# Gates, branch projections and values by tokens, 512 channels at a time

## The chip, the cores and the metric

One core of a Trainium2 chip. The metric is the device time of one execution in microseconds, median of several runs. The granted clock of TensorE is given as a share of 2.4 GHz; it was 0.991 on average over the profiled span, and 1.00 in every stretch that this text speaks of.

## The reference, cut to what matters

One layer of a decoder on 256 positions (T) of 1,024 channels (D), all in float32. The part that the change touches is the token mixer:

```python
qa, ka, va, qd, kd, vd, b_gate, c_gate, hc, gate_logits = jnp.split(
    x @ w_in, split_points, axis=-1)
y_moba = moba_attention(...)                     # 512 wide, values va: 512
y_conv = b_gate * causal_dwconv(c_gate * hc, w_short_conv)   # 512 wide
y_dil = dilated_mixture(...)                     # 256 wide, values vd: 768
gates = jax.nn.sigmoid(gate_logits).reshape(b, s, N_BRANCH, D_MODEL)
merged = (gates[:, :, 0] * (y_moba @ w_moba_proj)
          + gates[:, :, 1] * (y_conv @ w_conv_proj)
          + gates[:, :, 2] * (y_dil @ w_dil_proj))
return merged @ w_mix_out
```

Behind it come a residual with layer norm, an MLP with a gated convolution (w_up, w_down), and a second residual with layer norm. The change leaves these as they are.

## The kernel before, in words

Every weight is read once from memory, in blocks of 2,048 float32 per partition (1 MB; some branch blocks are smaller), on SyncE's DMA queue (`load_next`, L111) into three `raw` buffers. A block is cut into pieces of 128x512. Each float32 operand of a matrix product is split into two rounded parts, h and l (`split`, L148): ScalarE copies h (L149), VectorE subtracts to get l (L150). A product of two split operands is three passes on TensorE (`mm3`, L198 to 202: h·h, h·l, l·h). Pieces are split in the order of use, up to 10 ahead (`LEAD`); a new block is loaded when the last piece of a block has been split.

The program is written as a chain of groups. A group fills one accumulator bank (`acc`, three in rotation, L60) and ends with `tick` (L155), which splits further pieces, then has the bank emptied (`consume`), then issues one entry of the list `side` (attention work that is strung between the groups). A scheduler may shift instructions a little within an engine's row. In order of the program:

- queries and keys, by channels (`project`, L209): the weight's 128 columns stay in the array, the 256 tokens of transposed x (xTh, xTl) move through it;
- values (L462 to 464), by tokens (`project_tokens`, L218): 128 tokens of x stay, 256 columns of the weight move. Three groups of 256 channels for the dilated attention, two for MoBA;
- short convolution, MoBA queries and keys, with the attention in between;
- gates and branches (L504 to 529), by channels, in four quarters d of 256 channels. In each, the three gates are projected (L509: ScalarE writes the sigmoid), then for both halves c of 128 channels the three branches with `take(5)` pieces: VectorE multiplies the product with the gate (L523) and adds (L525). `late` splits the gated sum, which has channels on partitions and so can stay in the array for the next product as it is;
- output projection w_mix_out (L597 to 622), by tokens, products of 512 columns into five `att` banks, then residual and layer norm; then the MLP.

Of the kernel before, what the change touches and what calls it, by code (L numbers as in the profile page):

```python
# [7 lines left out]
F32 = mybir.dt.float32  # L8
F32R = mybir.dt.float32r
I32 = mybir.dt.int32  # L10
BF16 = mybir.dt.bfloat16
AF = mybir.ActivationFunctionType
# [25 lines left out]
def trunk(ctx: ExitStack, tc, x, w_in, w_short_conv, w_moba_proj, w_dil_proj, w_conv_proj, w_mix_out,  # L38
# [18 lines left out]
    def buf(dt=F32, shape=(P, 512)):  # L57
        return act.tile(list(shape), dt, tag="b2", name=fresh("b"), bufs=B2)

    def acc(shape=(P, 512)):  # L60
        return ps.tile(list(shape), F32, tag="acc", name=fresh("acc"), bufs=3)
# [8 lines left out]
    def block(*parts):  # L70

        blocks.append(parts)

    def kview(w, c0, c1, k0=0, k1=None):
        k1 = w.shape[0] // P if k1 is None else k1
        return w[k0 * P:k1 * P, c0:c1].rearrange("(k p) c -> p k c", p=P)

    def columns(base, n):
        for b in range(n):
            c = base + 256 * b  # L80
            block(kview(w_in, c, c + 256))

    columns(DIL_Q, 3)
    columns(DIL_K, 3)
    columns(DIL_V, 3)
    columns(MOBA_V, 2)
    for b in range(2):
        columns(CONV_C + 256 * b, 1)
        columns(CONV_H + 256 * b, 1)
        columns(MOBA_Q + 256 * b, 1)  # L90
        columns(MOBA_K + 256 * b, 1)
    columns(CONV_B, 2)
    for d in range(4):
        for g in range(3):
            columns(GATE + g * D + d * 256, 1)
        c = d * 256
        block(kview(w_dil_proj, c, c + 256))
        block(kview(w_conv_proj, c, c + 256), kview(w_moba_proj, c, c + 256))
    for b in range(4):
        block(kview(w_mix_out, 0, D, 2 * b, 2 * b + 2))  # L100
    for j in range(0, NJ + 2, 2):
# [40 lines left out]
    def take(n):  # L142

        i = used[0]
        assert len(ready) >= i + n, (len(ready), i, n)
        return ready[i:i + n]
# [8 lines left out]
    def tick(n, consume=None, ahead=1):  # L155


        used[0] += n
        while late:
            late.pop(0)()  # L160
        prep(n + ahead)
        if consume:
            consume()
        if side:
            side.pop(0)()
# [32 lines left out]
    def mm3(o, ah, al, bh, bl, first, last):  # L198

        nc.tensor.matmul(o, ah, bh, start=first, stop=False)  # L200
        nc.tensor.matmul(o, ah, bl, start=False, stop=False)  # L201
        nc.tensor.matmul(o, al, bh, start=False, stop=last)  # L202

    def cut(w, k, c0, c1):

        c = (k % 2) * 256
        return [t[:, c + c0:c + c1] for t in w[k // 2]]

    def project(consume, xh=xTh, xl=xTl, ahead=1):  # L209

        w = take(4)
        for c in range(2):
            o = acc((P, T))
            for k in range(KT):
                mm3(o, *cut(w, k, c * P, c * P + P), xh[:, k, :], xl[:, k, :], k == 0, k == KT - 1)
            tick(2, lambda: consume(c, o), ahead)

    def project_tokens():  # L218

        w = take(4)  # L220
        vh, vl = buf(F32R, (P, 2, 256)), buf(F32R, (P, 2, 256))
        for t in range(2):
            s = slice(t * P, (t + 1) * P)
            o = acc((P, T))
            for k in range(KT):
                mm3(o, xTh[:, k, s], xTl[:, k, s], *cut(w, k, 0, 256), k == 0, k == KT - 1)
            tick(2, lambda: split(o, vh[:, t, :], vl[:, t, :]))
        return vh, vl
# [230 lines left out]
    yd = [buf(F32R, (P, 2, T)) for _ in range(2)]  # L459
    p, q = (dilated(c, dq, dk, dv, [t[:, c, :] for t in yd]) for c in range(2))  # L460
    side += [p[0], p[1], p[2], q[0], p[3], p[4], q[1], p[5], q[2], p[6], q[3], q[4], q[5], q[6]]
    for g in range(3):  # L462
        dv.append(project_tokens())
    mv = [project_tokens() for b in range(2)]

    conv, ymT = [], []
    for b in range(2):
# [34 lines left out]


    merged = []  # L504
    for d in range(4):
        gs = []
        for g in range(3):
            s = buf(F32, (P, 2, T))
            project(lambda c, o: nc.scalar.activation(s[:, c, :], o, AF.Sigmoid))  # L509
            gs.append(s)  # L510
        assert not side
        m = gs[2]
        h, l = buf(F32R, (P, 2, T)), buf(F32R, (P, 2, T))
        w = take(5)
        for c in range(2):
            for g, k0, n, ys in ((2, 0, 2, [yd]), (1, 2, 4, ycT), (0, 6, 4, ymT)):
                o = acc((P, T))
                for k in range(n):
                    yh, yl = ys[k // 2]
                    mm3(o, *cut(w, k0 + k, c * P, c * P + P), yh[:, k % 2, :], yl[:, k % 2, :], k == 0, k == n - 1)  # L520

                def merge():
                    nc.vector.tensor_mul(gs[g][:, c, :], o, gs[g][:, c, :])  # L523
                    if g < 2:
                        nc.vector.tensor_add(m[:, c, :], m[:, c, :], gs[g][:, c, :])  # L525

                tick({(0, 2): 0, (0, 1): 1, (0, 0): 1, (1, 2): 1, (1, 1): 1, (1, 0): 1}[c, g], merge)
            late.append(lambda c=c, m=m, h=h, l=l: split(m[:, c, :], h[:, c, :], l[:, c, :]))
        merged.append((h, l))


    half_c = const.tile([P, 1], F32, name="half_c")
# [67 lines left out]
    for t in range(2):  # L600
        for c0, c1, p in mo[t]:
            for k in range(2):
                row_products(p, merged[0], w, k, t, c0, c1, k == 0, False)
        tick(2)
    wm = []
    for b in (1, 2, 3):
        while len(ready) < used[0] + 4:
# [124 lines left out]
```

## Time and profile before

| | |
|---|---|
| median of 3 runs | 479.36 us (479.05 to 480.07) |
| the profiled execution | 479.29 us, span of its instructions 477.5 us |
| instructions | 9,121, of them 3,582 products on TensorE |
| bytes read from memory | 81.9 MB, 174 GB/s over the span |

PE is TensorE's products, PEld its weight loads (they overlap), DVE is VectorE, ACT is ScalarE, SP is SyncE. Products on TensorE are pipelined: the length shown for one is longer than the step to the next, so the step from start to start is to be read.

### The profile page before, as it was taken

The numbers are of one execution on the slowest core, as the hardware profiler recorded it, in microseconds if no ns is written. First come the engines' busy times: TensorE is split into PE (matmuls) and PEld (weight loads), VectorE is DVE, ScalarE is ACT, GpSimd is POOL, SyncE is SP. The second block draws the span as 40 slices with busy tenths as digits, with TensorE's granted clock in tenths as the row PEclk, the third lists the DMA queues.
The fourth block names the chain that finished last, engine by engine and source line by source line (L and its number), as shares of the span: only waits on it lengthen the run. The fifth ranks groups of instructions, "written<-read, shape, count | busy, mean of one in ns | idle before, by whom it ended". The sixth has DMA issues, their size and how long they took to land.

```text
span 477.5 us, 9121 instructions
## 1 busy us (share of the span) xinstructions
PE 466.5 (98%) x3582; PEld 450.6 (94%) x3582; DVE 360.3 (75%) x775; ACT 271.0 (57%) x579; POOL 10.4 (2%) x29
## 2 busy tenths in 40 slices
PE   7999999999999999999999999999999999999993
PEld 4999999999999999999999899999999999999983
DVE  6788996778989757484748866997867676786966
ACT  4767774737668645454545316866555565564710
POOL 1100000010100000000000000000000000000000
PEclk8999999999999999999999999999999999999997
DMA  8986555254451745656465914657465545637002
GB/s 265 359 253 189 178 177 177 89 176 131 136 161 41 231 144 182 195 165 211 153 220 200 311 49 151 243 175 265 127 227 176 178 177 188 221 122 244 21 2 88
DMA packets 69502, 83.51 MB, mean 175 GB/s; under 512 B 1688, under 2 KB 64852, under 8 KB 69460
## 3 DMA queue, kind: packets, MB, share of 16 engines
q1 hardware_dynamic: 69460, 82.94, 53.3%
q8 instruction: 28, 0.46, 0.4%
q14 instruction: 14, 0.11, 0.1%
HBM read 81.89 MB, written 1.05 MB: 174 GB/s over the span
## 4 chain that ended last, share of the span: by engine, by line
PE 97%; DMA 1%; DVE 1%; SPq 0%; ACT 0%; issue 0%; DVEq 0%
PE acc L200 24%; PE acc L202 24%; PE acc L201 24%; PE att L201 7%; PE att L200 7%; PE att L202 7%; PE att L266 2%; PE acc L439 1%; PE att L287 1%; DMA xs<-in_x_dram 1%; PE att L194 0%; DVE r L551 0%; SPq L124 0%; SPq L177 0%; PE acc L594 0%
## 5 line engine op out<-in xcount | busy, mean ns | idle before, releaser
L150 DVE TENSOR_TENSOR b<-raw,b 128x512 fp32r<-128x512 f32 x300 | 196.1, 687 | 38.0 <-ACT b L149 35.6
L149 ACT CAST b<-raw 128x512 fp32r<-128x512 f32 x300 | 169.3, 620 | 6.2 <-DMA raw<-in_w_in_dram 2.9
L200 PE MATMUL acc<-xTh,b 128*128 128x256 f32 x432 | 122.9, 284 | 0.0
L201 PE MATMUL acc<-xTl,b 128*128 128x256 f32 x432 | 122.2, 283 | 0.0
L202 PE MATMUL acc<-xTh,b 128*128 128x256 f32 x432 | 122.2, 283 | 0.0
L200 PE MATMUL acc<-x1Th,b 128*128 128x256 f32 x320 | 90.9, 284 | 0.0
L202 PE MATMUL acc<-x1Th,b 128*128 128x256 f32 x320 | 90.6, 283 | 0.0
L201 PE MATMUL acc<-x1Tl,b 128*128 128x256 f32 x320 | 90.5, 283 | 0.0
L200 PEld LDWEIGHTS acc<-xTh,b 128*128 128x128 f32 x432 | 82.8, 192 | 0.2
L201 PEld LDWEIGHTS acc<-xTl,b 128*128 128x128 f32 x432 | 82.9, 192 | 0.0
L202 PEld LDWEIGHTS acc<-xTh,b 128*128 128x128 f32 x432 | 82.9, 192 | 0.0
L201 PEld LDWEIGHTS acc<-x1Tl,b 128*128 128x128 f32 x320 | 61.4, 192 | 0.1
L200 PEld LDWEIGHTS acc<-x1Th,b 128*128 128x128 f32 x320 | 61.4, 192 | 0.1
L202 PEld LDWEIGHTS acc<-x1Th,b 128*128 128x128 f32 x320 | 61.4, 192 | 0.0
L629 DVE SCALAR_TENSOR_TENSOR b<-acc,fconv,b 128x255 f32<-128x255 f32 x80 | 38.5, 481 | 30.2 <-ACT b L627 29.2
L200 PE MATMUL att<-b,b 128*128 128x512 f32 (+1 forms) x170 | 58.9, 347 | 0.0
L201 PE MATMUL att<-b,b 128*128 128x512 f32 (+1 forms) x170 | 58.9, 347 | 0.0
L202 PE MATMUL att<-b,b 128*128 128x512 f32 (+1 forms) x170 | 58.7, 345 | 0.0
L149 ACT CAST b<-b 128x256 fp32r<-128x256 f32 x34 | 13.8, 408 | 46.8 <-DVE b L525 23.4
L627 ACT ACTIVATE b<-acc,fconv 128x256 f32<-128x256 f32 x40 | 22.6, 565 | 28.6 <-PE acc L202 28.6
L200 PEld LDWEIGHTS att<-b,b 128*128 128x128 f32 x170 | 32.2, 189 | 4.0
L202 PEld LDWEIGHTS att<-b,b 128*128 128x128 f32 x170 | 32.1, 189 | 4.0
(108 smaller groups left out, 625.0 us busy)
## 6 DMA issues: line engine op xcount, KB each, us to landing
raw<-in_w_in_dram SPq DMA_DIRECT2D x31, 1024.0 KB, 5.7
raw<-in_w_up_dram SPq DMA_DIRECT2D x22, 1024.0 KB, 5.4
raw<-in_w_down_dram SPq DMA_DIRECT2D x11, 1024.0 KB, 5.0
raw<-in_w_mix_out_dram SPq DMA_DIRECT2D x4, 1024.0 KB, 5.3
raw<-in_w_in_dram SPq DMA_DIRECT2D x8, 256.0 KB, 6.2
raw<-in_w_conv_proj_dram SPq DMA_DIRECT2D x4, 512.0 KB, 3.5
raw<-in_w_moba_proj_dram SPq DMA_DIRECT2D x4, 512.0 KB, 4.6
xs<-in_x_dram SPq DMA_DIRECT2D x4, 256.0 KB, 3.6
```

The source lines that it names most:

```text
L149: nc.scalar.copy(h, src)
L150: nc.vector.tensor_sub(l, src, h.bitcast(F32))
L200: nc.tensor.matmul(o, ah, bh, start=first, stop=False)
L201: nc.tensor.matmul(o, ah, bl, start=False, stop=False)
L202: nc.tensor.matmul(o, al, bh, start=False, stop=last)
L266: nc.tensor.matmul(o, qt, k[i][:, a, :], start=i == 0, stop=i == 1)
L287: nc.tensor.transpose(p[:, i, :], b, ident)
L439: nc.tensor.matmul(o[c], w[i][:, s:s + P], xt[:, k, :], start=k + i == 0 and xt is xTh, stop=k == KT - 1 and i == 1)
L627: nc.scalar.activation(v, o, AF.Identity, bias=w[3], scale=w[0])
L629: nc.vector.scalar_tensor_tensor(v[:, j:], o[:, :T - j], w[j], v[:, j:], op0=OP.mult, op1=OP.add)
```

## The change

Three places go from 256 to 512 columns:

- `wide` lays a weight out as two blocks of four rows of 128 by 512 columns; a piece is then one row k with 512 columns, where it was two rows with 256.
- `by_tokens` takes the place of `project` for gates and branches, and of `project_tokens` for four of the five value groups: 128 tokens of the input stay in the array, 512 columns of the weight move. It fills two banks at once, one for each half of the tokens, k by k, and empties both after the last k. `project_tokens_half` is the old form for the fifth value group.
- Gates and branches run in two halves d of 512 channels. The gated sum now has tokens on partitions; `turn_m` transposes it (four transposes of 128x128 into an `att` bank for each half of the tokens) and splits it from there. It stands in `side`, so it is issued within the first groups of what comes next: the gates of the second half, and the output projection.

Counted over the program, 1,008 products of 256 columns become 504 of 512, and 16 transposes are added; 24 sigmoids of 128x256 become 12 of 128x512, 24 multiplications and 16 additions become 12 and 8 of 128x512.

```diff
--- before.py
+++ after.py
@@ -80,22 +80,28 @@
             c = base + 256 * b
             block(kview(w_in, c, c + 256))
 
+    def wide(base):
+
+        for k in (0, 4):
+            block(kview(w_in, base, base + 512, k, k + 4))
+
     columns(DIL_Q, 3)
     columns(DIL_K, 3)
-    columns(DIL_V, 3)
-    columns(MOBA_V, 2)
+    wide(DIL_V)
+    columns(DIL_V + 512, 1)
+    wide(MOBA_V)
     for b in range(2):
         columns(CONV_C + 256 * b, 1)
         columns(CONV_H + 256 * b, 1)
         columns(MOBA_Q + 256 * b, 1)
         columns(MOBA_K + 256 * b, 1)
     columns(CONV_B, 2)
-    for d in range(4):
+    for c in range(0, D, 512):
         for g in range(3):
-            columns(GATE + g * D + d * 256, 1)
-        c = d * 256
-        block(kview(w_dil_proj, c, c + 256))
-        block(kview(w_conv_proj, c, c + 256), kview(w_moba_proj, c, c + 256))
+            wide(GATE + g * D + c)
+        block(kview(w_dil_proj, c, c + 512), kview(w_conv_proj, c, c + 512, 0, 2))
+        block(kview(w_conv_proj, c, c + 512, 2, 4), kview(w_moba_proj, c, c + 512, 0, 2))
+        block(kview(w_moba_proj, c, c + 512, 2, 4))
     for b in range(4):
         block(kview(w_mix_out, 0, D, 2 * b, 2 * b + 2))
     for j in range(0, NJ + 2, 2):
@@ -215,7 +221,34 @@
                 mm3(o, *cut(w, k, c * P, c * P + P), xh[:, k, :], xl[:, k, :], k == 0, k == KT - 1)
             tick(2, lambda: consume(c, o), ahead)
 
+    def by_tokens(xs, n, consume, ahead=1):
+
+
+        o = [acc() for _ in range(2)]
+        for k in range(0, n, 2):
+            w = take(2)
+            for i in range(2):
+                xh, xl = xs(k + i)
+                for t in range(2):
+                    s = slice(t * P, (t + 1) * P)
+                    mm3(o[t], xh[:, s], xl[:, s], *w[i], k + i == 0, k + i == n - 1)
+            tick(2, (lambda: [consume(t, o[t]) for t in range(2)]) if k == n - 2 else None, ahead)
+
+    def of_x(k):
+        return xTh[:, k, :], xTl[:, k, :]
+
     def project_tokens():
+
+        vs = [(buf(F32R, (P, 2, 256)), buf(F32R, (P, 2, 256))) for _ in range(2)]
+
+        def consume(t, o):
+            for i, (vh, vl) in enumerate(vs):
+                split(o[:, 256 * i:256 * i + 256], vh[:, t, :], vl[:, t, :])
+
+        by_tokens(of_x, KT, consume)
+        return vs
+
+    def project_tokens_half():
 
         w = take(4)
         vh, vl = buf(F32R, (P, 2, 256)), buf(F32R, (P, 2, 256))
@@ -459,9 +492,9 @@
     yd = [buf(F32R, (P, 2, T)) for _ in range(2)]
     p, q = (dilated(c, dq, dk, dv, [t[:, c, :] for t in yd]) for c in range(2))
     side += [p[0], p[1], p[2], q[0], p[3], p[4], q[1], p[5], q[2], p[6], q[3], q[4], q[5], q[6]]
-    for g in range(3):
-        dv.append(project_tokens())
-    mv = [project_tokens() for b in range(2)]
+    dv.extend(project_tokens())
+    dv.append(project_tokens_half())
+    mv = project_tokens()
 
     conv, ymT = [], []
     for b in range(2):
@@ -502,31 +535,32 @@
 
 
     merged = []
-    for d in range(4):
+    for d in range(2):
         gs = []
         for g in range(3):
-            s = buf(F32, (P, 2, T))
-            project(lambda c, o: nc.scalar.activation(s[:, c, :], o, AF.Sigmoid))
+            s = [buf(F32), buf(F32)]
+            by_tokens(of_x, KT, lambda t, o: nc.scalar.activation(s[t], o, AF.Sigmoid))
             gs.append(s)
         assert not side
-        m = gs[2]
-        h, l = buf(F32R, (P, 2, T)), buf(F32R, (P, 2, T))
-        w = take(5)
-        for c in range(2):
-            for g, k0, n, ys in ((2, 0, 2, [yd]), (1, 2, 4, ycT), (0, 6, 4, ymT)):
-                o = acc((P, T))
-                for k in range(n):
-                    yh, yl = ys[k // 2]
-                    mm3(o, *cut(w, k0 + k, c * P, c * P + P), yh[:, k % 2, :], yl[:, k % 2, :], k == 0, k == n - 1)
-
-                def merge():
-                    nc.vector.tensor_mul(gs[g][:, c, :], o, gs[g][:, c, :])
-                    if g < 2:
-                        nc.vector.tensor_add(m[:, c, :], m[:, c, :], gs[g][:, c, :])
-
-                tick({(0, 2): 0, (0, 1): 1, (0, 0): 1, (1, 2): 1, (1, 1): 1, (1, 0): 1}[c, g], merge)
-            late.append(lambda c=c, m=m, h=h, l=l: split(m[:, c, :], h[:, c, :], l[:, c, :]))
-        merged.append((h, l))
+        h, l = ([buf(F32R, (P, 2, T)) for _ in range(2)] for _ in range(2))
+
+        def turn_m(t, gs=gs, h=h, l=l):
+            p = att((P, 4, P))
+            for i in range(4):
+                nc.tensor.transpose(p[:, i, :], gs[2][t][:, i * P:(i + 1) * P], ident)
+            for i in range(2):
+                split(p[:, 2 * i:2 * i + 2, :], h[i][:, :, t * P:(t + 1) * P], l[i][:, :, t * P:(t + 1) * P])
+
+        for g, n, ys in ((2, 2, [yd]), (1, 4, ycT), (0, 4, ymT)):
+
+            def merge(t, o):
+                nc.vector.tensor_mul(gs[g][t], o, gs[g][t])
+                if g < 2:
+                    nc.vector.tensor_add(gs[2][t], gs[2][t], gs[g][t])
+
+            by_tokens(lambda k: [y[:, k % 2, :] for y in ys[k // 2]], n, merge)
+        side += [lambda f=turn_m: f(0), lambda f=turn_m: f(1)]
+        merged.extend(zip(h, l))
 
 
     half_c = const.tile([P, 1], F32, name="half_c")
@@ -602,6 +636,7 @@
             for k in range(2):
                 row_products(p, merged[0], w, k, t, c0, c1, k == 0, False)
         tick(2)
+    assert not side
     wm = []
     for b in (1, 2, 3):
         while len(ready) < used[0] + 4:
```

Two places in the rows of the engines. `mm3` is L200 to 202 in the kernel before and L206 to 208 in the changed one.

TensorE, from the end of one gate to the start of the next, before (acc573 is the last bank of gate 1, acc580 the first of gate 2; xT is x, b are weights):

```order
L200 MATMUL acc573_3090<-xTh_95,b545_2934 128x256
L201 MATMUL acc573_3090<-xTl_96,b545_2934 128x256
L202 MATMUL acc573_3090<-xTh_95,b546_2935 128x256
L200 MATMUL acc580_3127<-xTh_95,b549_2955 128x256 [waits Activation_49]
L201 MATMUL acc580_3127<-xTl_96,b549_2955 128x256
L202 MATMUL acc580_3127<-xTh_95,b550_2956 128x256
```

The same place in the change, first half (acc439 and acc440 are gate 0's banks for the two halves of the tokens, acc462 and acc463 gate 1's):

```order
L206 MATMUL acc440_2227<-b416_2134,xTh_95 128x512
L207 MATMUL acc440_2227<-b417_2135,xTh_95 128x512
L208 MATMUL acc440_2227<-b416_2134,xTl_96 128x512
L206 MATMUL acc462_2334<-b426_2192,xTh_95 128x512
L207 MATMUL acc462_2334<-b427_2193,xTh_95 128x512
L208 MATMUL acc462_2334<-b426_2192,xTl_96 128x512
L206 MATMUL acc462_2334<-b428_2196,xTh_95 128x512
L207 MATMUL acc462_2334<-b429_2197,xTh_95 128x512
L208 MATMUL acc462_2334<-b428_2196,xTl_96 128x512
L206 MATMUL acc462_2334<-b441_2242,xTh_95 128x512 [waits Activation_49]
L206 MATMUL acc463_2335<-b426_2192,xTh_95 128x512 [waits Activation_49]
L207 MATMUL acc463_2335<-b427_2193,xTh_95 128x512
```

The products are 512 wide with the weight as the moving operand. The second bank of the new gate waits for ScalarE, which has to empty acc439 (the same bank) first; four more products of the first bank have been drawn ahead of it.

VectorE, in the branches of the last quarter, before (b635, b623, b610 are gates 2, 1, 0; L150 rows with raw are weight splits of w_mix_out):

```order
L523 TENSOR_TENSOR b623_3375<-acc650_3527,b623_3375 128x256 [waits PE_49]
L525 TENSOR_TENSOR b635_3446<-b635_3446,b623_3375 128x256 [waits DVE_49]
L523 TENSOR_TENSOR b610_3300<-acc653_3546,b610_3300 128x256 [waits PE_49]
L525 TENSOR_TENSOR b635_3446<-b635_3446,b610_3300 128x256 [waits DVE_49]
L523 TENSOR_TENSOR b635_3446<-acc656_3565,b635_3446 128x256 [waits PE_49,Activation_49]
L150 TENSOR_TENSOR b648_3518<-b635_3446,b647_3517 128x256 [waits Activation_49]
L150 TENSOR_TENSOR b658_3575<-raw620_3368,b657_3574 128x512 [waits Activation_49]
L523 TENSOR_TENSOR b623_3375<-acc660_3581,b623_3375 128x256 [waits PE_49]
L150 TENSOR_TENSOR b662_3595<-raw632_3439,b661_3594 128x512 [waits DMAHW0_49,Activation_49]
L525 TENSOR_TENSOR b635_3446<-b635_3446,b623_3375 128x256 [waits DVE_49]
```

And in the change, second half (b583 and b584 are gate 2 of the two halves of the tokens, b561 and b562 gate 1; L557 multiplies, L559 adds, L156 splits weights):

```order
L557 TENSOR_TENSOR b583_2839<-acc610_2935,b583_2839 128x512 [waits PE_49]
L557 TENSOR_TENSOR b584_2840<-acc611_2936,b584_2840 128x512 [waits PE_49]
L156 TENSOR_TENSOR b619_2974<-raw591_2863,b618_2973 128x512 [waits DVE_49,Activation_49]
L156 TENSOR_TENSOR b621_2978<-raw591_2863,b620_2977 128x512 [waits DVE_49,Activation_49]
L156 TENSOR_TENSOR b624_2996<-raw600_2905,b623_2995 128x512 [waits DMAHW5_49,DVE_49,Activation_49]
L156 TENSOR_TENSOR b626_3000<-raw600_2905,b625_2999 128x512 [waits DVE_49,Activation_49]
L156 TENSOR_TENSOR b630_3022<-raw600_2905,b629_3021 128x512 [waits DVE_49,Activation_49]
L156 TENSOR_TENSOR b632_3026<-raw600_2905,b631_3025 128x512 [waits DVE_49,Activation_49]
L156 TENSOR_TENSOR b635_3044<-raw605_2927,b634_3043 128x512 [waits DMAHW6_49,DVE_49,Activation_49]
L557 TENSOR_TENSOR b561_2748<-acc616_2959,b561_2748 128x512 [waits PE_49]
L557 TENSOR_TENSOR b562_2749<-acc617_2960,b562_2749 128x512 [waits PE_49]
L559 TENSOR_TENSOR b583_2839<-b583_2839,b561_2748 128x512 [waits DVE_49]
```

The multiplications come in pairs of double width, and between the pair of the dilated branch (acc610, acc611) and that of the convolution (acc616, acc617) stand seven weight splits, where single ones stood.

## Rows read from the trace of the kernel before

**Rows 1.** The page, parts 1, 2, 4: busy us (share); tenths by slice; chain.

```profile
PE 466.5 (98%) x3582; PEld 450.6 (94%) x3582; DVE 360.3 (75%) x775; ACT 271.0 (57%) x579; POOL 10.4 (2%) x29
...
PE   7999999999999999999999999999999999999993
...
PEclk8999999999999999999999999999999999999997
...
PE 97%; DMA 1%; DVE 1%; SPq 0%; ACT 0%; issue 0%; DVEq 0%
```

**Rows 2.** Busy time by stretch: values, gates with branches, output projection.

```profile
core 0: us, PE busy (x) PEld busy (x) DVE busy (x) ACT busy (x) POOL busy (x), PEclk, DMA share, GB/s
46.00:100.00 54.00, 54.00 (x440) 53.22 (x438) 44.90 (x112) 35.01 (x78) 1.23 (x4) 1.00 0.52 163
...
172.00:256.60 84.60, 84.60 (x707) 84.60 (x707) 52.34 (x101) 41.06 (x86) 0.00 (x0) 1.00 0.56 180
256.60:278.00 21.40, 21.40 (x116) 18.55 (x116) 19.60 (x36) 8.67 (x17) 0.92 (x1) 1.00 0.76 246
```

**Rows 3.** Groups by line and shape: count, busy us, mean ns, idle before.

```profile
L200 PE MATMUL acc<-xTh,b 128*128 128x256 f32 x432 | 122.9, 284 | 0.0
...
L200 PE MATMUL att<-b,b 128*128 128x512 f32 x100 | 39.1, 391 | 0.0
...
L200 PE MATMUL acc<-b,xTh 128*128 128x256 f32 x80 | 22.8, 285 | 0.0
...
L200 PE MATMUL acc<-b,b 128*128 128x256 f32 x80 | 22.6, 283 | 0.0
...
L523 DVE TENSOR_TENSOR b<-acc,b 128x256 f32<-128x256 f32 x24 | 10.1, 422 | 6.9 <-PE acc L202 6.6
...
L509 ACT ACTIVATE b<-acc 128x256 f32<-128x256 f32 x24 | 9.2, 385 | 24.5 <-PE acc L202 24.4
```

**Rows 4.** TensorE by time (start, length), values; 34 like rows between.

```profile
99.76 0.28 PE L202 MATMUL acc<-xTh,b 128*128 128x256 f32 x1
...
103.96 0.28 PE L201 MATMUL acc<-xTl,b 128*128 128x256 f32 x1
```

**Rows 5.** TensorE by time, output projection; 41 like rows between.

```profile
264.71 0.39 PE L202 MATMUL att<-b,b 128*128 128x512 f32 x1
...
274.23 0.39 PE L202 MATMUL att<-b,b 128*128 128x512 f32 x1
```

**Rows 6.** TensorE by time, attention values: three wide products; then a narrow one.

```profile
76.52 0.40 PE L200 MATMUL att<-b,b 128*128 128x512 f32 x1
...
77.22 0.28 PE L200 MATMUL att<-b,b 128*128 128x256 f32 x1
```

**Rows 7.** TensorE by time: twelve attention transposes and the two products behind them.

```profile
64.49 1.47 PE L287 MATMUL att<-ident,e 128*128 128x128 f32 x12
65.72 0.36 PE L200 MATMUL acc<-b,xTh 128*128 128x256 f32 x1
65.92 0.28 PE L201 MATMUL acc<-b,xTh 128*128 128x256 f32 x1
```

**Rows 8.** Waits: us in total, times, longest.

```profile
ACT b L509 <- PE acc L202: 24.4, 21, 2.6
...
DVE b L523 <- PE acc L202: 6.6, 10, 1.0
...
ACT b L149 <- DMA raw<-in_w_up_dram: 2.5, 2, 1.7
```

**Rows 9.** ScalarE and VectorE by time: four weight splits behind each other.

```profile
241.29 2.17 ACT L149 CAST b<-raw 128x512 fp32r<-128x512 f32 x4
...
247.70 2.50 DVE L150 TENSOR_TENSOR b<-raw,b 128x512 fp32r<-128x512 f32 x4 [3.26 <-ACT b L149]
```

**Rows 10.** TensorE and VectorE by time, end of the last branches.

```profile
256.53 0.28 PE L202 MATMUL acc<-b,b 128*128 128x256 f32 x1
...
257.67 0.42 DVE L523 TENSOR_TENSOR b<-acc,b 128x256 f32<-128x256 f32 x1
```

## The prediction

> **What bounds the kernel now.** I read the page first for who is on the chain, then the stretches that the change touches, then single rows for the price of one instruction. The page [rows 1] leaves no doubt on the bound: TensorE is busy 98% of the span, every slice between the first and the last shows 9 tenths, and the chain that ended last is 97% TensorE. In the stretches of the values (46 to 100 us) and of gates and branches (172 to 256.6 us) TensorE is busy for the whole stretch at a granted clock of 1.00, which is the 2.4 GHz level, while VectorE is busy for 83% and 62% of it and the DMA engines for about half [rows 2]. So a change is worth here what it takes from the row of TensorE instructions, less any gap that it opens in that row. Busy time misleads on the price of one: a 256-wide product is shown with 284 ns and a 512-wide one with 391 ns [rows 3], but they overlap. What counts is the step from one start to the next.
>
> **The price of a product.** 256-wide: from 99.76 to 103.96 us stand 36 products, 35 steps in 4.20 us, 0.1200 us each [rows 4]. 512-wide, in the output projection: from 264.71 to 274.23 us stand 43, 42 steps in 9.52 us, 0.2267 us each [rows 5]. Two narrow products cost 0.2400 us, one wide product with the same columns 0.2267, so 13.3 ns go with the instruction and not with its columns. The nearest row on the dear side is a run of three wide products between narrow ones, 76.52 to 77.22 us, 0.2333 each [rows 6]. The new stages are long rows of wide products that alternate between two banks, like the output projection's first 12, so I take 0.2267 and keep 0.2333 as the other end.
>
> The Trainium skill (TensorE: Matmul & The Clock Gate, section "Back-to-back issue gap") puts the step of a warm matmul at its columns over 2.4 GHz plus about 2.5 ns. By it the halved count would be worth 504 x 2.5 ns = 1.26 us, an estimate from that page. By that rule a 256-wide step would be 109 ns; the trace's 120 ns [rows 4] disagrees, so the sum does without it.
>
> **The change part by part.** It turns 1,008 products of 256 columns into 504 of 512: 192 in the values (four of the five 256-column groups, 48 products each), 576 in the gates (12 groups of 48) and 240 in the branches (4 x 60). Multiplications and weights are the same.
> - Products: 1,008 x 0.1200 = 120.96 us against 504 x 0.2267 = 114.24 us, 6.72 us less (values 1.28, gates 3.84, branches 1.60). At 0.2333 it would be 117.6 us, 3.4 us less. All of it is on the chain.
> - Added: 16 transposes of 128x128 (two halves, two token rows, four each). Twelve attention transposes take 1.23 us from 64.49 to the next product at 65.72, and that one's follower is 0.08 us late at 65.92: 1.31 / 12 = 0.109 us each [rows 7]. 16 x 0.109 = 1.75 us more, on the chain. Without the lag it is 1.64 us.
> - Switches of width around the attention work that is strung between the k steps of the values: 0.01 to 0.03 us each, about six, 0.1 us.
> - ScalarE and VectorE: 24 sigmoids of 256 columns become 12 of 512; 24 multiplications and 16 additions become 12 and 8 of double width; 8 splits of the gated sum move from the summed tile to the transposed bank, two per transposed bank. About the same work, and neither engine is the bound. DMAs: the weight blocks keep their size and queue, rows get 2 KB instead of 1 KB; nothing is moved past them.
> - Added wait of the output projection: it needs the transposed sum. The order puts the first half's transposes into the next gate, and the second half's behind 12 products of the output projection and behind most of its first token row. VectorE then has two 256-column subtractions more before the norm of the first token row; each is about 0.42 us by the nearest form, L523 [rows 3]. Uncovered that would be 0.84 us. I take 0, since those matrix products between still follow.
>
> **The hand-over of the banks** is the one new risk. There are three acc banks. Before, one group filled one bank while two stood for eviction. Now a group fills two banks at once, and the next group's second bank is the first bank of the group before. That bank is full three products before the group's end and is wanted three products after it: 6 x 0.2267 = 1.36 us for the eviction, where a bank used to have two whole groups. There are 12 such places (six gates, six branches); in the values the narrow group and the projections around them take banks that were filled long before.
> - Gates (ScalarE alone empties the bank): in the kernel before ScalarE stood waiting for TensorE ahead of 21 of 24 sigmoids [rows 8], so its queue is empty when a bank fills. A 512-wide sigmoid I estimate at 0.65 us, from the weight copies of that width [rows 9]. It ends when the group ends, 0.7 us before the bank is wanted. The order even shows four further products ahead of the first such place.
> - Branches (VectorE): here it has no such slack. It waited for TensorE ahead of only 10 of 24 multiplications [rows 8], and the last of them began at 257.67 us, about 1.0 us after its group's last product, started at 256.53, was through [rows 10]. So I counted the order of the second half by hand, from the end of its third gate as 0. ScalarE: sigmoids to 0.65, then copies at 0.52 each ((2.17 - 0.62) / 3) [rows 9]. VectorE: two subtractions behind them, to 2.4, then the multiplication of the dilated branch (0.7, the width of a weight subtraction), to 3.1; its bank is wanted at 2.72 + 0.68 = 3.40. Second multiplication to 3.7, seven weight subtractions at 0.60 each ((2.50 - 0.69) / 3) [rows 9], to 7.9; the conv bank has been full since 7.5; multiplication to 8.6; wanted at 8.16 + 4 x 0.2267 = 9.07, since the order drew one product ahead of it. The moba bank is full at 12.9, emptied at 13.6, wanted at 14.3.
> So every hand-over is covered, the thinnest (dilated to conv, conv to moba, in both halves) by 0.3 to 0.5 us. For errors in four thin covers I add 0.3 us. If all four covers were missed by as much as they hold, it would be 1.6 us.
>
> **The sum.** -6.72 + 1.75 + 0.1 + 0.3 = -4.57 us. The profiled execution took 479.29 us (span 477.5), the median of the runs is 479.36, so both give **474.7 us**. Best end: the transposes without their lag, no wait at hand-overs, less switching: -6.72 + 1.64 = -5.1, 474.2; half a microsecond below for the spread of runs gives 473.6. Dear end: products 3.4 less instead of 6.72 gives 478.0; four missed covers on the cheap sum give 476.0.
>
> **The rivals.**
> - Hand-overs leak: a wait of 0.1 to 0.25 us at each of the 12, or some tenths more at the six of VectorE. 1.2 to 3 us go back: 475.6 to 477.4, centre 476.4. For it: VectorE's lateness before [rows 10]. Against it: the covers counted above.
> - Hand-overs fail (the slower side): VectorE reaches the multiplication of a full bank three more weight subtractions late, 3 x 0.60 = 1.8 us. The bank is then empty 1.8 + 0.7 us after it was full, 1.1 us after it is wanted; six branches lose 6.8 us, and 479.29 - 4.87 + 6.8 = 481.2. It decides from 4.87 / 6 = 0.81 us of wait per branch on. VectorE's 62% in that stretch [rows 2] speaks against it.
> - The instruction's share is not saved: the price of a pass goes with its columns in the new stages, 0.2400 us for a wide product. Then 504 x 0.24 = 120.96 us, nothing saved, and the transposes remain: 479.29 + 1.75 + 0.1 = 481.1. Against it: the same shape with the same kinds of operands has 0.2267 in the output projection [rows 5]. By the page's 2.5 ns it would be 479.29 - 1.26 + 1.85 = 479.9, no change.
> - Weights come no faster: the gates want a 1 MB block each 24 x 0.2267 = 5.44 us instead of 48 x 0.12 = 5.76. If DMA were at its limit with the 180 GB/s of that stretch, only the values would gain: 479.29 - 1.28 + 0.1 = 478.1. Against it: 246 GB/s in the next stretch [rows 2], and 2.5 us of waiting for w_up weights in all [rows 8].
>
> **How the numbers follow.** Forecast 0.78, leaking hand-overs 0.12, failing hand-overs 0.03, no saving per instruction 0.02, its small form of no change 0.01, weights 0.02, something not seen 0.02. Range: 473.6 to 477.0 takes in the forecast and most of the leak, and leaves out about 0.15. A measurement of this kernel tells 0.2% (about 1 us) from no change, so faster is below 478.4: 0.92; within 0.2%: 0.03; slower: 0.05.
>
> **What would show it.** In the changed profile the gates and branches are rows of 512-wide products at 0.227 us from start to start, TensorE has some 3,100 instructions and stays at 98%. If the hand-overs leak, TensorE waits for L557 (multiplication) or L542 (sigmoid) appear with tenths of a microsecond each. If the transposes are dearer, L550 shows a step over 0.11 us. I am wrong if the wide step is not 0.227 there, or if TensorE shows gaps of more than 2 us in sum that it didn't have.

## The result and the profile after

The changed kernel takes 474.43 us (median of 4 runs, 473.81 to 474.49), the kernel before 479.21 us in the runs beside it; the ratio is 0.9895, 95% interval 0.9878 to 0.9912. That is 4.8 us less, by the interval 4.2 to 5.8; forecast were 474.7 us and 4.6 us less. The profiled execution took 473.81 us, its span is 472.0 us.

The page of the changed kernel, parts 1 and 4, beside [rows 1]:

```profile
PE 461.5 (98%) x3094; PEld 424.2 (90%) x3094; DVE 355.7 (75%) x755; ACT 268.2 (57%) x567; POOL 10.4 (2%) x29
...
PE 96%; DMA 1%; DVE 1%; SPq 1%; issue 0%; ACT 0%; DVEq 0%
```

TensorE has 488 instructions fewer (504 products less, 16 transposes more) and is as full as before: the span became shorter because the row did, not because a gap closed. The windows from the first transposes of the small weights to the last branch product, and from there to the first transposes of x1 behind the output projection (columns as in [rows 2]):

```profile
32.30:250.10 217.80, 217.80 (x1343) 196.00 (x1343) 163.11 (x378) 129.53 (x290) 2.45 (x8) 1.00 0.54 174
250.10:272.70 22.60, 22.60 (x123) 19.22 (x122) 19.18 (x36) 8.88 (x18) 0.92 (x1) 1.00 0.57 185
```

TensorE is busy for the whole of both, at a granted clock of 1.00, as it was in [rows 2]. Against the 21.4 us of before the second one grew by some 1.2 us: here a part of the gain was given back, and the experiments have to tell what of it is the transposes.

Spans compare badly here, because they contain the start of the kernel, which the change doesn't touch and which moves by itself: the transposes of the small weights began between 32.4 and 36.5 us in the nine profiled executions of this case. Windows from 8 to 12 us, the kernel before, then the changed one:

```profile
8.00:12.00 4.00, 4.00 (x22) 4.00 (x23) 2.54 (x5) 2.33 (x4) 0.00 (x0) 0.59 1.06 356
```

```profile
8.00:12.00 4.00, 3.65 (x33) 3.45 (x31) 3.44 (x6) 2.39 (x5) 0.00 (x0) 1.00 1.08 357
```

In the one execution the granted clock was 0.59 there, in the other 1.00. The text ahead of the prediction gives 1.00 for every stretch that it speaks of; that doesn't hold for this one. The drop is no matter of the change: of the executions with wide gates e2, e6 and e7 show 0.54, 0.59 and 0.50 in the same window, e1, e3 and e4 show 1.00. So I read the time between rows that every kernel has. TensorE by time, kernel before (start, length), and then the changed kernel; the last branch product of before, at 256.53 us, is in [rows 10]:

```profile
33.62 0.23 PE L423 MATMUL att<-ident,b 12*128 12x12 f32 x1
...
278.05 0.49 PE L594 MATMUL acc<-ident,x 128*128 128x128 f32 x3
```

```profile
32.47 0.23 PE L456 MATMUL att<-ident,b 12*128 12x12 f32 x1
...
249.88 0.39 PE L208 MATMUL acc<-b,b 128*128 128x512 f32 x1
...
272.72 0.49 PE L628 MATMUL acc<-ident,x 128*128 128x128 f32 x3
```

To the last branch product it is 222.91 us before and 217.41 after, 5.50 less; from there to the transposes of x1 21.52 and 22.84, 1.32 more. Together 4.18 us less. From there to the last product it is 191.71 and 191.69 us, no difference; with it the whole is 4.20 us less. The same three rows, read in every run:

| us between the rows | to the last branch product | from there to x1 | together |
|---|---|---|---|
| before | 222.91 | 21.52 | 244.43 |
| after | 217.41 | 22.84 | 240.25 |
| e1, narrow products | 223.78 | 24.48 | 248.26 |
| e2, no transposes | 216.46 | 21.60 | 238.06 |
| e3, other bank | 217.41 | 22.52 | 239.93 |
| e4, two acc banks | 224.25 | 21.15 | 245.40 |
| e5, values only | 221.77 | 21.52 | 243.29 |
| e6, gates and branches only | 218.55 | 22.72 | 241.27 |
| e7, bank emptied first | 217.41 | 22.52 | 239.93 |

In e4 the first two columns are cut at another place of the work: six wide products of the output projection (1.36 us) stand there among the second half's branches. Counted where the other kernels have them, its columns are 222.89 and 22.51. TensorE by time, the first of the six, e4:

```profile
248.73 0.39 PE L206 MATMUL att<-b,b 128*128 128x512 f32 x1
```

The wide products in the second half's gates, TensorE by time; five steps behind the transposes, then 23 in a settled row (rows between left out):

```profile
209.46 0.39 PE L207 MATMUL acc<-b,xTh 128*128 128x512 f32 x1
...
210.62 0.39 PE L206 MATMUL acc<-b,xTh 128*128 128x512 f32 x1
...
215.84 0.39 PE L208 MATMUL acc<-b,xTl 128*128 128x512 f32 x1
```

The last 23 steps take 5.22 us, 0.2270 each, the price taken from [rows 5]. The first five take 1.16 us, 0.232 each, near the dear end of [rows 6].

### The profile page after: what moved, and what is told of

It reads as the page before. It is cut to its first block, busy times and chain, and to the rows that moved or that the text cites. A ratio compares the mean times of both kernels' runs of the same rounds, so it can differ in the third digit from the quotient of the medians.

```text
span 472.0 us, 8122 instructions
## 1 busy us (share of the span) xinstructions
PE 461.5 (98%) x3094; PEld 424.2 (90%) x3094; DVE 355.7 (75%) x755; ACT 268.2 (57%) x567; POOL 10.4 (2%) x29
## 4 chain that ended last, share of the span: by engine, by line
PE 96%; DMA 1%; DVE 1%; SPq 1%; issue 0%; ACT 0%; DVEq 0%
PE acc L206 24%; PE acc L208 24%; PE acc L207 24%; PE att L206 7%; PE att L207 7%; PE att L208 7%; PE att L299 2%; PE att L320 1%; DMA xs<-in_x_dram 1%; PE acc L472 1%; PE att L550 0%; SPq L130 0%; SPq L183 0%; DVE r L585 0%; PE acc L628 0%
## 5 line engine op out<-in xcount | busy, mean ns | idle before, releaser
L156 DVE TENSOR_TENSOR b<-raw,b 128x512 fp32r<-128x512 f32 x300 | 193.8, 684 | 43.4 <-ACT b L155 41.4
L155 ACT CAST b<-raw 128x512 fp32r<-128x512 f32 x300 | 167.6, 619 | 7.3 <-DMA raw<-in_w_in_dram 4.8
L206 PE MATMUL acc<-x1Th,b 128*128 128x256 f32 x320 | 90.9, 284 | 0.0
L206 PE MATMUL acc<-xTh,b 128*128 128x256 f32 x240 | 68.5, 285 | 0.0
L207 PE MATMUL acc<-xTl,b 128*128 128x256 f32 x240 | 67.9, 283 | 0.0
L208 PE MATMUL acc<-xTh,b 128*128 128x256 f32 x240 | 67.9, 283 | 0.0
L206 PEld LDWEIGHTS acc<-x1Th,b 128*128 128x128 f32 x320 | 61.4, 192 | 0.1
L206 PE MATMUL att<-b,b 128*128 128x512 f32 (+1 forms) x170 | 59.1, 348 | 0.0
L206 PE MATMUL acc<-b,xTh 128*128 128x512 f32 (+1 forms) x144 | 54.7, 381 | 0.0
L207 PE MATMUL acc<-b,xTh 128*128 128x512 f32 (+1 forms) x144 | 54.4, 378 | 0.0
L208 PE MATMUL acc<-b,xTl 128*128 128x512 f32 (+1 forms) x144 | 54.4, 378 | 0.0
L206 PEld LDWEIGHTS acc<-xTh,b 128*128 128x128 f32 x240 | 46.0, 192 | 0.2
L207 PEld LDWEIGHTS acc<-xTl,b 128*128 128x128 f32 x240 | 46.0, 192 | 0.0
L208 PEld LDWEIGHTS acc<-xTh,b 128*128 128x128 f32 x240 | 46.0, 192 | 0.0
```

What stands on the lines that cost most here:

```text
L155: nc.scalar.copy(h, src)
L156: nc.vector.tensor_sub(l, src, h.bitcast(F32))
```

## The experiments

Each is set against the kernel before on the same chip: 479.34 us for e1 to e4, 479.17 for e5 to e7. All but e5 are edits of the changed kernel.

**e1: is it the number of products?** The wide product is issued as two narrow ones into the halves of the same bank. Order, banks, transposes, blocks and evictions stay; only the 504 products come back.

```diff
-                    mm3(o[t], xh[:, s], xl[:, s], *w[i], k + i == 0, k + i == n - 1)
+                    for c in (0, 256):
+                        mm3(o[t][:, c:c + 256], xh[:, s], xl[:, s], *(v[:, c:c + 256] for v in w[i]), k + i + c == 0,
+                            k + i == n - 1 and c == 256)
```

> The changed kernel with each 512-wide product of by_tokens issued as two products of 256 columns into the two halves of its bank; weight layout, banks, evictions and transposes stay as changed. If the gain is the 13.3 ns that go with each instruction, 504 more of them cost 504 x 13.3 ns = 6.7 us: 474.4 + 6.7 = 481.1 us, slower than the kernel before, with starts 0.12 us apart. If the gain comes from anything else that came with the change (2 KB rows in the weight loads, wider evictions, the layout by tokens), it stays: below 477 us.

Measured: 482.61 us, ratio 1.0064 (1.0051 to 1.0078). The gain is gone, and more than that: it is 8.2 us above the changed kernel and 3.3 above the one before. TensorE by time in a gate of e1, 42 rows between:

```profile
175.80 0.28 PE L206 MATMUL acc<-b,xTh 128*128 128x256 f32 x1
...
180.96 0.28 PE L207 MATMUL acc<-b,xTh 128*128 128x256 f32 x1
```

43 steps in 5.16 us, 0.1200 each, in the new order and with the same operands. So 0.240 against 0.227 us for the same columns: the difference goes with the instruction. Each product has its own weight load, and e1 brings both back (PEld x3598 against x3094), so the 13 ns are those of the pair; no run here separates the two. That part is 504 x 0.013 = 6.5 us; the stretch up to the last branch product, which holds all of them, is 6.37 us longer than in the changed kernel. The forecast 481.1 left 1.5 us of the time unexplained, and the trace has them in the main in one place, at the second of the second half's two transposed banks. All engines by time, e1:

```profile
271.60 0.39 PE L208 MATMUL att<-b,b 128*128 128x512 f32 x1
271.70 1.14 ACT L155 CAST b<-raw 128x512 fp32r<-128x512 f32 x2 [3.88 <-DMA raw<-in_w_up_dram]
272.35 0.69 DVE L156 TENSOR_TENSOR b<-raw,b 128x512 fp32r<-128x512 f32 x1 [2.91 <-ACT b L155]
272.96 1.28 DVE L573 SCALAR_TENSOR_TENSOR x<-xs,att 128x512 f32<-128x512 f32 x2
273.69 0.42 PEld L552 LDWEIGHTS att<-ident,b 128*128 128x128 f32 x4 [2.12 <-DVE x L573]
273.69 0.66 PE L552 MATMUL att<-ident,b 128*128 128x128 f32 x4 [1.70 <-DVE x L573]
```

From the bottom up: the transposes (L552) wait for VectorE's residual (L573), because that empties the `att` bank which they are to fill. The residual stands in VectorE's row behind one weight subtraction (L156), which waits for ScalarE's copy (L155), which waited 3.88 us for a block of w_up to land. TensorE starts nothing for 2.09 us where a step would be 0.23: 1.86 us lost. The same rows of the changed kernel:

```profile
263.10 1.14 ACT L155 CAST b<-raw 128x512 fp32r<-128x512 f32 x2 [2.15 <-DMA raw<-in_w_up_dram]
...
263.75 0.69 DVE L156 TENSOR_TENSOR b<-raw,b 128x512 fp32r<-128x512 f32 x1 [1.19 <-ACT b L155]
...
264.36 1.28 DVE L571 SCALAR_TENSOR_TENSOR x<-xs,att 128x512 f32<-128x512 f32 x2
...
264.73 0.39 PE L208 MATMUL att<-b,b 128*128 128x512 f32 x1
265.09 0.42 PEld L550 LDWEIGHTS att<-ident,b 128*128 128x128 f32 x4 [0.40 <-DVE x L571]
265.09 0.66 PE L550 MATMUL att<-ident,b 128*128 128x128 f32 x4
```

Here the chain is the same, but TensorE comes to it late enough: the transposes start 0.36 us behind the last product, 0.13 more than a step. The prediction knew nothing of this chain. Counted with it, e1 fits: 6.5 + 1.86 - 0.13 = 8.2 us above the changed kernel (8.2 by the medians, 8.0 between the rows of the table). The copy of the block began 14.87 us behind the last branch product in e1 (256.83 us) and 13.22 in the changed kernel; why the block landed later there was not tried.

**e2: what do the transposes cost?** The split reads the gated sum itself in place of a transposed bank; the transposition is left out, everything else stays.

```diff
-            p = att((P, 4, P))
-            for i in range(4):
-                nc.tensor.transpose(p[:, i, :], gs[2][t][:, i * P:(i + 1) * P], ident)
+            p = gs[2][t].rearrange("p (a c) -> p a c", c=P)
```

> The changed kernel without its 16 transposes: the gated sum is split as it is, tokens on partitions, so this run leaves out the transposition and the output projection multiplies the wrong operand. If a transpose costs its step of 0.109 us and nothing else, 16 of them are 1.75 us: 472.7 us. The changed profile also shows some 0.3 us of gaps around the transposes of the output projection, which would go with them: 472.4 us. If the transposes fill gaps that are there anyway, the time stays at 474.4 us.

Measured: 472.25 us, ratio 0.986 (0.9838 to 0.9883), 2.18 us below the changed kernel; by the trace 240.25 - 238.06 = 2.19. One group of four in the changed kernel, TensorE by time:

```profile
205.60 0.60 PE L550 MATMUL att<-ident,b 128*128 128x128 f32 x4
...
205.96 0.48 PE L206 MATMUL acc<-b,xTh 128*128 128x512 f32 x1
...
206.27 0.39 PE L207 MATMUL acc<-b,xTh 128*128 128x512 f32 x1
```

Four transposes take 0.36 us, and the step behind them is 0.31 instead of 0.23: 0.44 in all, 0.11 each, as priced from [rows 7]. Four groups are 1.76 us. The other 0.4 us that e2 saves is the bank chain, which falls away with the bank, and dearer first steps behind each group. The Trainium skill (TensorE: Matmul & The Clock Gate, section "Part 4: PE-mode transpose") gives about 275 ns for a 128x128 bf16 transpose in a kernel's context; 16 of those, one after the other, would be 4.4 us, an estimate from that page, and e2 would have been near 470. The trace agrees on the length of one and not on that sum. The changed kernel's transposes, count, busy us and mean ns:

```profile
L550 PE MATMUL att<-ident,b 128*128 128x128 f32 x16 | 2.5, 276 | 0.0
```

One is shown with 276 ns, but they overlap, and the step in a row is what counts.

**e3: the chain taken away.** The second half's transposes go to an `acc` bank, which is free by then, since the output projection's sums hold all five `att` banks.

```diff
-        def turn_m(t, gs=gs, h=h, l=l):
-            p = att((P, 4, P))
+        def turn_m(t, gs=gs, h=h, l=l, bank=acc if d else att):
+            p = bank((P, 4, P))
```

> The changed kernel with the second half's transposed banks taken from acc instead of att. In the changed order the second of them waits until a bank of the output projection has been emptied (VectorE's residual), since five of the five att banks are taken. If the gaps near 265 to 267 us come from that bank, they close and 0.2 to 0.3 us are gained: 474.2 us, a difference that only the trace can show. If they come from the transposes themselves, the trace shows them again at the new place and the time is the same.

Measured: 474.08 us, ratio 0.989 (0.9872 to 0.9908). Against the changed kernel's 474.43 that is inside the scatter; the trace tells more. TensorE by time:

```profile
255.94 0.28 PE L208 MATMUL att<-b,b 128*128 128x256 f32 x1
...
256.06 0.60 PE L550 MATMUL acc<-ident,b 128*128 128x128 f32 x4
...
256.42 0.48 PE L206 MATMUL att<-b,b 128*128 128x512 f32 x1
```

The transposes now follow the first token row's products with a step of 0.12 us, nine microseconds earlier, and wait for nothing; the stretch up to x1 is 22.52 instead of 22.84 us. So the chain cost 0.32 us in the changed kernel: 0.13 ahead of the late transposes, the rest in dearer steps from there to 267.78 us. e4 confirms it: with a sixth `att` bank nothing waits there either, and the stretch, counted alike, is 22.51 us.

**e4: how thin is the cover of the hand-overs?** One bank moves from `acc` to `att`. With two banks the next group's first bank is the one that the group before had full three products before its end; in the changed kernel that bank is the next group's second, wanted three products later.

```diff
-        return ps.tile(list(shape), F32, tag="acc", name=fresh("acc"), bufs=3)
+        return ps.tile(list(shape), F32, tag="acc", name=fresh("acc"), bufs=2)
...
-        return ps.tile(list(shape), F32, tag="att", name=fresh("att"), bufs=5)
+        return ps.tile(list(shape), F32, tag="att", name=fresh("att"), bufs=6)
```

> The changed kernel with two acc banks and six att banks instead of three and five, so that each group finds the banks of the group just before it: the cover of an eviction falls from six products (1.36 us) to three (0.68 us). If the hand-overs are as counted, the gates (0.65 us for a sigmoid) still just fit, 0 to 0.1 us each, and the branches wait 0.4 us twice in each half, about 2 us in the two halves with gates and branches; other stages with narrow groups may lose more, some 1 to 3 us. So 476 to 479 us. If eviction was never near the path, nothing changes there: 474.4 us. If it fails wholly, each of 12 places waits a microsecond or more: above 486 us.

Measured: 484.72 us, ratio 1.0117 (1.0093 to 1.014), far above what was expected, and 10.3 us above the changed kernel. The hand-overs are one part of that. ScalarE's at the end of a gate and VectorE's at the end of the first half's dilated branch, e4 (184.21 us is the step behind the last product into the gate's first bank):

```profile
184.21 0.39 PE L206 MATMUL acc<-b,xTh 128*128 128x512 f32 x1
...
184.47 1.22 ACT L542 ACTIVATE b<-acc 128x512 f32<-128x512 f32 x2 [5.82 <-PE acc L208]
...
185.12 0.19 PEld L206 LDWEIGHTS acc<-b,xTh 128*128 128x128 f32 x1 [0.49 <-ACT b L542]
...
198.79 1.31 DVE L557 TENSOR_TENSOR b<-acc,b 128x512 f32<-128x512 f32 x2
...
199.54 0.50 PE L206 MATMUL acc<-b,b 128*128 128x512 f32 x1 [0.17 <-DVE b L557]
```

ScalarE had waited 5.82 us for the bank, so it was there the moment the bank was full, and with 0.68 us of cover TensorE still waits: from 184.21 to 185.12 us it takes 0.91 us until the next product into that bank starts. That is more than the sigmoid's 0.6 us (1.22 for two); it doesn't fit into 0.68 and does fit into 1.36. Nine of the twelve places show such gaps, 0.27 to 0.44 us each with the late step behind them, 3.06 us together. The second half's branches show none, but that doesn't show that 0.68 us was enough there: two of their hand-overs had three products of the output projection each as further cover, and behind the third no group takes `acc` banks. The rest of e4's loss lies elsewhere. Between the profiled executions it is 11.1 us: beside the 3.06, 4.0 in the start, 2.3 between the small weights and the first gate, 2.0 behind the transposes of x1, less the 0.3 of the late transposes. Other projections fill `acc` banks too, and at the start this met the clock. Windows of e4 (start and end of the stretch, then as in [rows 2]), and TensorE by time there:

```profile
14.80:19.00 4.20, 2.07 (x18) 1.89 (x17) 3.37 (x7) 3.57 (x8) 0.00 (x0) 1.00 1.08 368
19.00:22.40 3.40, 3.40 (x18) 3.40 (x18) 2.07 (x5) 1.14 (x4) 0.00 (x0) 0.51 1.06 368
```

```profile
17.57 0.36 PE L206 MATMUL acc<-xTh,b 128*128 128x256 f32 x1 [2.13 <-DVE b L273]
...
19.07 0.39 PE L206 MATMUL acc<-xTh,b 128*128 128x256 f32 x1
...
22.46 0.31 PE L207 MATMUL acc<-xTl,b 128*128 128x256 f32 x1
```

TensorE waited 2.13 us for VectorE to empty a bank (L273), went on at the full clock for some 1.5 us, and then ran at 0.51, the 1.2 GHz level, for 3.4 us: 16 steps from 19.07 to 22.46 us take 3.39 us, 0.212 each where 0.12 is usual, 1.5 us more. The wait and what followed it make 3.6 of the 4.0 us by which this execution reached the small weights later than the changed kernel's (36.49 against 32.47 us). The expectation had 1 to 3 us for the other stages with narrow groups; what it lacked is this wait at the start with the clock behind it, and the sigmoids' way from a full bank to a free one.

**e5 and e6: do the parts add up?** e5 is the kernel before with only the values made wide; e6 the changed kernel with the old values. The layout of the weight blocks goes with each and is cut here, as are the helpers.

```diff
-    for g in range(3):
-        dv.append(project_tokens())
-    mv = [project_tokens() for b in range(2)]
+    dv.extend(project_tokens())
+    dv.append(project_tokens_half())
+    mv = project_tokens()
```

```diff
-    dv.extend(project_tokens())
-    dv.append(project_tokens_half())
-    mv = project_tokens()
+    for g in range(3):
+        dv.append(project_tokens_half())
+    mv = [project_tokens_half() for b in range(2)]
```

> The kernel before with only the values changed: 192 narrow products become 96 wide ones, no transposes, no new hand-over. By the step 96 x 13.3 ns = 1.28 us, less 0.1 us for switches of width: 1.2 us faster, ratio 0.9975, about 478.1 us. If VectorE's eviction of two banks at once (eight halves in a row behind the attention work) holds TensorE up, nothing or a loss.

> The changed kernel with the old values: gates and branches wide, transposes in. By the step 408 x 13.3 ns = 5.44 us less 1.75 us for the transposes and 0.4 us for the gaps that the changed profile shows: 3.3 us faster, ratio 0.993, about 475.9 us. The two parts should add up to the whole change (4.5 to 4.8 us); if they don't, one works through the other.

Measured: e5 478.28 us, ratio 0.9978 (0.9966 to 0.999); e6 475.77 us, ratio 0.9938 (0.9921 to 0.9955). Both within 0.2 us of what was expected. By the rows of the table above e5 gains 1.14 us and e6 3.16, together 4.30 against 4.18 for the whole: the parts add, and neither pays for the other.

**e7: a better order at the one leak?** e3, and in `by_tokens` the eviction of both banks is written ahead of `tick` and so ahead of the weight splits that it issues.

```diff
-            tick(2, (lambda: [consume(t, o[t]) for t in range(2)]) if k == n - 2 else None, ahead)
+            if k == n - 2:
+                for t in range(2):
+                    consume(t, o[t])
+            tick(2, None, ahead)
```

> The changed kernel with the transposed banks of the second half from acc, and with a wide group's banks emptied ahead of the weight splits of that step instead of behind them. By the hand-over account one visible gap (0.10 us, first half, dilated branch to conv) goes, with those near 265 us: 0.3 to 0.4 us, 474.0 us, at the edge of what can be measured. If evictions ahead of the splits make weights late instead, TensorE waits for splits and it is slower than 474.4 us.

Measured: 474.75 us, ratio 0.9915 (0.9897 to 0.9933), no gain over e3 or the changed kernel; between the rows of the table it is the same as e3, 239.93 us. The leak is still there. All engines by time, e7:

```profile
194.36 1.29 DVE L560 TENSOR_TENSOR b<-acc,b 128x512 f32<-128x512 f32 x2
...
195.10 0.19 PEld L206 LDWEIGHTS acc<-b,b 128*128 128x128 f32 x1 [0.27 <-DVE b L560]
```

The multiplication began 0.74 us before the product that needs its bank, as in the changed kernel 0.75 (191.77 and 192.52 us, below). Where the eviction stands in the program did not move it: VectorE's row has the same order there, two weight subtractions and then the pair of multiplications. That the scheduler set this order is likely and not shown.

## Why the prediction held, step by step

**The price of a product** held. A wide step is 0.2270 us in the new stages, a narrow one 0.1200 in e1, and e1 takes the whole gain back. By the Trainium skill's rule of columns over 2.4 GHz and about 2.5 ns (TensorE: Matmul & The Clock Gate, "Back-to-back issue gap", which gives it for the gap of an isolated product) the 504 products would have been worth 1.26 us, an estimate from that page. Against that rule stand 6.5 us in the steps of e1. What was a little off is the first steps behind every interruption: 0.232 us instead of 0.227, which the sum had only as 0.1 us for switches.

**The transposes** held: 0.44 us for four, 1.76 us for all, against 1.75.

**The hand-overs** held, with one exception, and the allowance of 0.3 us was generous; the covers themselves were counted too thick. VectorE and TensorE of the changed kernel by time, first half, from the dilated branch to the convolution's:

```profile
189.11 0.39 PE L206 MATMUL acc<-b,b 128*128 128x512 f32 x1
...
191.06 0.69 DVE L156 TENSOR_TENSOR b<-raw,b 128x512 fp32r<-128x512 f32 x1
...
191.77 1.29 DVE L557 TENSOR_TENSOR b<-acc,b 128x512 f32<-128x512 f32 x2
...
192.52 0.19 PEld L206 LDWEIGHTS acc<-b,b 128*128 128x128 f32 x1 [0.27 <-DVE b L557]
192.52 0.50 PE L206 MATMUL acc<-b,b 128*128 128x512 f32 x1
...
192.85 0.40 PE L207 MATMUL acc<-b,b 128*128 128x512 f32 x1
```

The multiplication (L557) came behind a weight subtraction; the weight load stood 0.27 us, and the step behind is 0.33 instead of 0.23 us. This is one of the four places that were named as thinnest, and it costs 0.10 us. The count by hand had the multiplication begin 2.4 us behind the end of the gate; here it began 2.66 us behind it (the gate's end is the start of the first branch product, 189.11 us), and that took the 0.3 us of cover away. The eleven others show no gap. In the changed kernel ScalarE and VectorE still waited for TensorE ahead of evictions, as in [rows 8]:

```profile
ACT b L542 <- PE acc L208: 27.9, 6, 5.5
...
DVE b L557 <- PE acc L208: 1.8, 2, 0.9
```

That the cover is needed is e4's part: with half of it nine places leak, all six of ScalarE's among them, which the count had called safe by 0.7 us. From a full bank to the next product it is 0.91 us there, where the count had 0.65 for the sigmoid alone, so in the changed kernel those places are safe by about 0.45 us (an estimate, 1.36 less 0.91).

**The two subtractions ahead of the norm**, taken at nothing, cost nothing that shows: in e3 the stretch from the last branch product to x1 is 1.00 us longer than before, of which 0.88 are the eight transposes in it; e2, which has the subtractions and no transposes, is 0.08 us longer there.

**What the sum lacked** is the bank of the last transposes. The prediction asked who needs the transposed sum and who splits it, and not which bank it goes to: the order puts it behind the output projection's products, when those hold all five `att` banks, so it became dependent on a residual, a weight split and the landing of a w_up block. It cost 0.32 us here (e3); in e1, where the block landed later, TensorE lost 1.86 us at it. That the changed kernel kept clear of such a loss was luck as far as the forecast goes; how late a block would have to land for it was not tried.

| term | forecast, us | by the trace, us |
|---|---|---|
| values, with switches | -1.18 | -1.14 (e5) |
| products of gates and branches | -5.44 | -5.30 (408 x 0.0130; -5.34 is left of e6's -3.16) |
| transposes | +1.75 | +1.76 |
| hand-overs | +0.3 | +0.10 |
| bank of the last transposes | not in it | +0.32 (e3) |
| sum | -4.57 | -4.26; between like rows -4.20 (e5 and e6: -4.30) |

The medians say 4.78 us less, the trace 4.20 from the small weights to the last product, and the lower end of the interval is 4.2. What the profiled executions differ in beside that is the start: they reached the small weights at 33.62 and 32.47 us, 1.15 us apart, on work that the change leaves alone, with the clock at 0.59 in the one and at 1.00 in the other. How much of the medians' 0.58 us is scatter of that start stays open. The sign, the size and the mechanism were right; that the forecast met the median to 0.3 us is partly that scatter.

The rivals fell each by a row: hand-overs that leak or fail by one gap of 0.10 us instead of 1.2 to 6.8; no saving per instruction by 0.2270 against 2 x 0.1200 and by e1; weights that come no faster by e6, which gains 3.16 us in the stage that they would have held.

## What to carry to other kernels

Where TensorE's row is the bound, count its instructions: here each, with its weight load, costs 13 ns beside its columns, so a wide product instead of two narrow ones pays 13 ns, and four transposes to turn the result back cost 0.44 us, or 33 products. One gate's bank has only 24 products and would not pay for its own transposes; three gates and three branches that end in one sum, 102 products, do. When a product is added late in a stage, ask not only who reads it but which bank it fills, who empties that bank, and what stands ahead of that in the emptying engine's row; a step that looks free can hang on a transfer.

## What the runs showed of the hardware

- The clock at the start: in e4 it fell to the 1.2 GHz level some 1.5 us after a wait of 2.13 us and stayed there for 3.4 us with TensorE busy all the while. In the kernel before, TensorE waited 1.64 us for x at 7.88 us and the clock was 0.59 from 8 to 12 us; in the changed kernel no wait there was over 0.79 us, and it stayed at 1.00. The length of the longest wait does not sort the nine executions: e4 waited 1.61 us for x at 7.81 us and shows 1.00 from 8 to 12 us, e6 waited no more than 0.90 us and shows 0.59. What decides it stays open. TensorE by time, the kernel before and then the changed one; then the windows of e4 and e6:

```profile
7.88 1.11 PE L194 MATMUL att<-ident,xs 128*128 128x128 f32 x4 [1.64 <-DMA xs<-in_x_dram]
```

```profile
7.70 0.66 PE L200 MATMUL att<-ident,xs 128*128 128x128 f32 x4 [0.79 <-DMA xs<-in_x_dram]
```

```profile
8.00:12.00 4.00, 3.42 (x29) 3.21 (x29) 2.74 (x5) 2.34 (x4) 0.00 (x0) 1.00 1.07 362
```

```profile
8.00:12.00 4.00, 3.78 (x21) 3.49 (x20) 3.08 (x5) 2.35 (x4) 0.00 (x0) 0.59 1.08 359
```

- Behind an interruption the next wide steps cost 0.31 and then about 0.232 us before they settle at 0.2270, so that a gap costs more than its length; at e4's places the late step adds some 0.1 us to gaps of 0.16 to 0.35.
- An engine that had waited 5.82 us for a bank needs more than 0.68 us from full to free for a 128x512 sigmoid of 0.6 us: 0.91 us from the start of the step behind the bank's last product to the start of the next product into it (e4), and no more than 1.36 us (no gap in the changed kernel).
